# Norm's factor moved from the MLP's up projection to its down projection's sums, in a two-layer encoder trunk

## The chip, the cores and the metric

The kernel runs on one core of a Trainium2 chip. The metric is the device time of one execution in microseconds, as the median of several runs. The engines are TensorE (PE; its weight loads are listed apart as PEld), VectorE (DVE), ScalarE (ACT), GpSimd (POOL) and SyncE (SP), which only issues transfers.

## The reference, cut to what matters

Two layers, each an attention (of different kinds) and an MLP, on 768 tokens of 1024 features; then a last Norm. The MLP is the part that the change touches:

```python
def rmsnorm(x, g, eps=NORM_EPS):
    xf = x.astype(jnp.float32)
    y = xf * lax.rsqrt(jnp.mean(xf * xf, axis=-1, keepdims=True) + eps)
    return (y * g.astype(jnp.float32)).astype(x.dtype)
...
        h = rmsnorm(x, ln_mlp[layer])
        x = x + jnp.square(jax.nn.relu(h @ w_up[layer])) @ w_down[layer]
    return rmsnorm(x, ln_f)
```

The up projection goes from 1024 to 4096 features, the down projection back. Norm's factor, call it R, is one positive number for each token. So relu(R u) squared is R squared times relu(u) squared, and a factor of a token can be taken through the down projection, which sums over features.

## The kernel before, in words

**Layout and arithmetic.** Everything lies with features on the 128 partitions and tokens along the free axis: x is 8 tiles of 128 x 768. `A` is the first half of the tokens, `B` the second, 384 each. Each fp32 operand is split in a high and a low half (`wsplit`, L76 to L81, for weights: ScalarE copies the high half `whi`, VectorE subtracts for `wlo`; `halve`, L114 to L120, for the other operand), and each product is made as three matmuls: high times high, high times low, low times high.

**Seven products for eight.** Both projections multiply 2 x 2 blocks by a scheme of the Strassen-Winograd kind: seven products of sums of blocks, and sums of the products afterwards. `comb` holds the sums of x for the up projection: 0 to 3 are plain blocks (`first`, L799), 4 to 7 sums (`second`, L804).

**Up projection** (L899 to L955). 16 steps over `mp`, each with 256 of the 4096 features. The first two are made with eight plain products, since the sums are not ready; in the others `weights` (L825) loads two tiles `wraw` (three buffers), GpSimd makes four sums of weights (L846), and the halves go through four buffers each of `whi` and `wlo`. The seven products go in the order 1, 3, 2, 6, 4, 7, 5 (L931 to L951); VectorE folds them from PSUM into `z` (L941 to L953). Then `finish` (L875): VectorE makes relu and the multiplication by R in one pass over 128 x 1536 (L880), ScalarE squares (L882), VectorE makes the sums of the four blocks of z that the down projection's products need (`t`, L889 to L891), and ScalarE's and GpSimd's queues store them to a DRAM tensor `T` (L883, L893). Norm's squares and their sum over features (`nm.add`, L141) come at the start, `rstd` (L155) and the spread of R over the partitions (L170) after the first blocks; so `finish` of the first two blocks waits until step 2.

**Down projection** (L959 to L1057). 28 steps: seven products in the order 1, 2, 7, 4, 5, 6, 3 (`ORDER`, L965), each over four groups `i` of features; a step has 48 matmuls into four PSUM banks (r = 0 to 3, L1022). SyncE loads weight blocks three steps ahead (`fetch`, L972), tiles that are kept and changed by later sums in pool `ch`, the others in `wd`, some in `wraw`. GpSimd adds a new block to a kept one for products 7, 5, 6 and 3 (`sums`, L987), two steps ahead; `halves` (L993) splits them one step ahead. `operand` (L920) reads a block of T back and splits it. After the last step of a product its four banks are folded into x, which holds the residual (L1029 to L1048); `u` keeps products 1 + 6.

**Behind it.** In layer 0 the next layer's split and Norm squares follow (L1061 to L1069). In layer 1 `final` (L1071) makes the last Norm for one half of the tokens while product 3 runs and for the other half at the end.

**Order.** The program text gives priorities; a scheduler orders each engine's instructions before the run by its own estimate of times and by which buffers are free. Each engine then runs its list strictly in that order, so an instruction that waits holds up all behind it on its engine.

Of the kernel before, what the change touches and what calls it, by code (L numbers as in the profile page):

```python
# [11 lines left out]
F32 = mybir.dt.float32  # L12
# [25 lines left out]
def kernel(ctx: ExitStack, tc: tile.TileContext, a: dict, y: bass.AP):  # L38
# [735 lines left out]
    def mlp(layer, src, o, x, es):  # L774
# [6 lines left out]
        sq = lambda: xo_tile("sq")  # L781
        two = [0]

        def sq2():
            two[0] ^= 1
            return xo_tile("sq") if two[0] else cpool.tile([P, NT], F32, tag="R", name="sq", bufs=1)

        nm = Norm(sq2)
# [82 lines left out]
        R, wait, done = [], [], list(range(FF // 256))  # L871

        T = [dram.tile([P, 7, ND, HT], F32, name=f"T{layer}_{i}") for i in range(NG)]

        def finish(z):  # L875
# [4 lines left out]
            nc.vector.scalar_tensor_tensor(out=z, in0=z, scalar=0.0, in1=R[0][:, None, :].broadcast_to([P, 2, NT]),  # L880
                                           op0=ALU.max, op1=ALU.mult)
            nc.scalar.activation(z, z, AF.Square)  # L882
# [17 lines left out]
        for k in MO:  # L900
            nm.add(x[k])
        for w in ws:
            z = ztile()
            pss = [bank(n) for n in (1, 6, 2, 4)]
            for last, bs in enumerate((((0, 0, 1), (0, 0, 0), (1, 1, 2), (1, 1, 3)), ((0, 1, 2), (0, 1, 3), (1, 0, 1), (1, 0, 0)))):
                for n, (i, j, c) in enumerate(bs):
                    product(pss[n], w[i, j], c, last == 0, last == 1)
                if last == 0 and wait:
                    rt = nm.rstd()
            for n, (i, sl) in enumerate(((0, B), (0, A), (1, B), (1, A))):  # L910
                nc.scalar.activation(z[:, i, sl], pss[n], AF.Copy)  # L911
            wait.append(z)
            if len(wait) == 1:
                w2 = weights()
                second()
        R.append(nm.spread(rt))
# [11 lines left out]
        for mp in range(2, FF // 256):  # L928
            w = weights() if mp > 2 else w2
# [6 lines left out]
            if mp == FF // 256 - 1:  # L936
# [3 lines left out]
                ths = [operand(1, 0)]  # L940
            add(z12, one(6), z11)  # L941
            add(z11, p2, z11)
            if mp == 2:
                finish(wait.pop(0))
# [4 lines left out]
            if mp == 2:  # L949
# [3 lines left out]
            add(z12, p5, z12)  # L953
            finish(z)
        g2s.close()  # L955
# [43 lines left out]
        def fold(out, x_, op=ALU.add):  # L999
            add(out, out, x_, op)  # L1000

# [6 lines left out]
        for s, (n, i) in enumerate(steps):  # L1008
# [20 lines left out]
            if i == NG - 1:  # L1029
                for r, ps in enumerate(banks):  # L1030
                    x12, x11, x22, x21 = (xb(r, m_, sl) for m_ in PR for sl in (A, B))
                    if n == 1:
                        nc.scalar.activation(u[:, r], ps, AF.Copy)
                    if n in (1, 2):
                        fold(x11, ps)
                    if n == 4:
# [221 lines left out]
```

## Time and profile before

| | us |
|---|---|
| three runs | 1743.85, 1742.30, 1744.41 |
| median | 1743.85 |
| profiled execution, its own time | 1743.15 |
| its span, first to last instruction | 1741.4 |
| up projection, layer 0 (first to last matmul of L861) | 361.8 to 610.3 |
| down projection, layer 0 (L1027) | 610.2 to 847.6 |
| up projection, layer 1 | 1238.4 to 1488.1 |
| down projection, layer 1 | 1487.9 to 1728.1 |

In the lines below, a group reads: line, engine, operation, output<-inputs, shapes, count | busy time in us, mean ns of one | idle time of the engine ahead of them, and what ended it. A timeline line reads: start, length in us, instruction, and in brackets the idle time before it and what ended that. A row of windows reads: stretch, length, busy time and number of instructions for PE, PEld, DVE, ACT and POOL, TensorE's granted clock as a share of full speed, the transfer engines' busy share, GB/s.

### The profile page before, as it was taken

Reading aid. Unit: us, or ns where it says so; the run is one execution under the profiler, and the core shown is the slowest. Engines: PE = TensorE matmul, PEld = TensorE weight load, DVE = VectorE, ACT = ScalarE, POOL = GpSimd, SP = SyncE. Lnnn points to the kernel's source line nnn. Section 1 sums busy time; section 2 is a strip of 40 time slices with the busy share of each in tenths; the row PEclk is TensorE's granted clock in tenths of the full one; section 3 lists DMA queues with packets and bytes.
Section 4 is the critical chain, followed back from the end, with each engine's and each line's share of the span. In section 5 each row is a group of like instructions: output and inputs, shape, how many; then the busy total and the mean of one; then the engine's idle time right before and its main releaser. Section 6 shows DMA issues by size and latency. Waiting matters only on the chain.

```text
span 1741.4 us, 28288 instructions
## 1 busy us (share of the span) xinstructions
PE 1710.9 (98%) x10988; PEld 1622.0 (93%) x10988; DVE 1396.1 (80%) x2202; ACT 823.5 (47%) x1513; POOL 571.3 (33%) x435
## 2 busy tenths in 40 slices
PE   8999999999999999999999999999999999999997
PEld 8888888899999999999999999988999999999997
DVE  8888647499888888899566776775898898787994
ACT  7765434354333354444435555554543333544442
POOL 2200000034566414574021222210235655054751
PEclk9999999999999999999999999999999999999998
DMA  4111222414444687663310111112134445977621
GB/s 170 37 46 49 69 78 91 136 38 156 158 158 157 199 343 300 244 209 133 115 49 32 50 39 33 55 59 97 49 117 160 159 168 177 345 294 266 207 91 73
DMA packets 74597, 235.42 MB, mean 135 GB/s; under 512 B 7904, under 2 KB 25056, under 8 KB 74464
## 3 DMA queue, kind: packets, MB, share of 16 engines
q1 hardware_dynamic: 52480, 186.93, 31.4%
q0 software_dynamic: 7168, 25.17, 3.9%
q10 hardware_dynamic: 14816, 21.52, 3.4%
q8 instruction: 86, 1.41, 0.3%
q14 instruction: 47, 0.39, 0.1%
HBM read 182.47 MB, written 50.33 MB: 134 GB/s over the span
## 4 chain that ended last, share of the span: by engine, by line
PE 69%; DVE 19%; issue 6%; ACT 4%; POOL 1%; DMA 1%; POOLq 0%; DVEq 0%; ACTq 0%; SPq 0%
PE dn L1027 26%; PE dqk L196 8%; PE opa L208 5%; DVE z L880 4%; PE dvp L196 4%; DVE z L869 3%; DVE wlo L81 3%; PE npa L208 3%; PE opb L208 3%; DVE t L869 3%; DVE t L797 2%; ACT z L882 2%; PE ds L274 2%; PE dpv L721 2%; PE qp L196 2%
## 5 line engine op out<-in xcount | busy, mean ns | idle before, releaser
L861 PE MATMUL up<-c,whi 128*128 128x384 f32 x1824 | 467.3, 337 | 1.3 <-ACT z L911 1.3
L1027 PE MATMUL dn<-th,whi 128*128 128x384 f32 x1792 | 460.8, 338 | 0.0
L861 PEld LDWEIGHTS up<-c,whi 128*128 128x128 f32 x1824 | 330.3, 188 | 1.6 <-ACT z L911 1.5
L1027 PEld LDWEIGHTS dn<-th,whi 128*128 128x128 f32 x1792 | 325.7, 188 | 0.7 <-DVE th L117 0.5
L861 PE MATMUL up<-c,wlo 128*128 128x384 f32 x912 | 309.8, 340 | 4.9 <-DVE wlo L81 4.7
L1027 PE MATMUL dn<-th,wlo 128*128 128x384 f32 x896 | 302.9, 338 | 0.5 <-DVE wlo L81 0.5
L846 POOL TENSOR_TENSOR s<-wraw 128x512 f32<-128x512 f32 x56 | 104.1, 1877 | 420.3 <-DMA wraw<-in_w_up_dram 369.6
L991 POOL TENSOR_TENSOR ch<-ch,wd 128x1024 f32<-128x1024 f32 x60 | 189.1, 3161 | 117.0 <-DVE wlo L81 94.5
L81 DVE TENSOR_TENSOR wlo<-ch,whi 128x1024 fp32r<-128x1024 f32 x88 | 167.2, 1915 | 27.7 <-ACT whi L80 27.5
L861 PEld LDWEIGHTS up<-c,wlo 128*128 128x128 f32 x912 | 171.3, 188 | 12.4 <-DVE wlo L81 12.1
L80 ACT ACTIVATE whi<-ch 128x1024 fp32r<-128x1024 f32 x88 | 93.2, 1064 | 176.2 <-PE dn L1027 138.9
L1027 PEld LDWEIGHTS dn<-th,wlo 128*128 128x128 f32 x896 | 168.3, 188 | 1.1 <-DVE wlo L81 1.1
L117 DVE TENSOR_TENSOR th<-tr,th 128x1536 fp32r<-128x1536 f32 x56 | 142.3, 2544 | 12.0 <-ACT th L116 11.5
L81 DVE TENSOR_TENSOR wlo<-wraw,whi 128x1024 fp32r<-128x1024 f32 (+3 forms) x132 | 139.2, 1055 | 14.3 <-ACT whi L80 14.1
L80 ACT ACTIVATE whi<-wraw 128x1024 fp32r<-128x1024 f32 (+3 forms) x128 | 116.8, 914 | 55.3 <-PE opb L208 24.6
L882 ACT ACTIVATE z<-z 128x1536 f32<-128x1536 f32 x32 | 47.7, 1490 | 165.8 <-DVE z L880 165.8
L196 PE MATMUL dqk<-whi,xh 128*128 128x256 f32 x384 | 114.7, 299 | 0.0
L196 PE MATMUL dqk<-whi,xl 128*128 128x256 f32 x384 | 107.5, 280 | 0.0
L196 PE MATMUL dqk<-wlo,xh 128*128 128x256 f32 x384 | 107.2, 279 | 0.0
L706 ACT ACTIVATE de<-ds,m 128x512 f32<-128x512 f32 (+1 forms) x96 | 58.4, 613 | 81.7 <-DVE m L704 81.7
L116 ACT ACTIVATE th<-tr 128x1536 fp32r<-128x1536 f32 x56 | 82.7, 1477 | 23.2 <-DMA tr<-T 14.1
L869 DVE TENSOR_TENSOR z<-up,z 128x384 f32<-128x384 f32 x168 | 89.7, 548 | 0.1
(220 smaller groups left out, 3736.4 us busy)
## 6 DMA issues: line engine op xcount, KB each, us to landing
wd<-in_w_down_dram SPq DMA_DIRECT2D x84, 512.0 KB, 5.0
tr<-T SPq DMA_DIRECT2D x56, 768.0 KB, 5.6
wraw<-in_w_up_dram SPq DMA_DIRECT2D x64, 512.0 KB, 3.6
T<-t POOLq DMA_DIRECT2D x64, 384.0 KB, 3.0
T<-z ACTq DMA_DIRECT2D x32, 576.0 KB, 3.0
ch<-in_w_down_dram SPq DMA_DIRECT2D x28, 512.0 KB, 7.4
wraw<-in_w_in_o_dram SPq DMA_DIRECT2D x24, 512.0 KB, 3.6
wraw<-in_w_in_e_dram SPq DMA_DIRECT2D x16, 512.0 KB, 3.6
```

What stands on the lines that cost most here:

```text
L80: nc.scalar.activation(hi, raw, AF.Copy)
L81: nc.vector.tensor_tensor(out=lo, in0=raw, in1=hi.bitcast(F32), op=ALU.subtract)
L116: nc.scalar.activation(hi, src, AF.Copy)
L117: nc.vector.tensor_tensor(out=lo, in0=src, in1=hi.bitcast(F32), op=ALU.subtract)
L196: nc.tensor.matmul(ps[:, :256], st[:, tk], col(k, part, 0, 256), start=(k == 0 and i == 0), stop=(k == KD - 1 and i == 2))
L208: nc.tensor.matmul(ps[:, : e - s], w, mv[:, s:e], start=(k == 0 and i == 0), stop=(k == nk - 1 and i == 2))
L846: nc.gpsimd.tensor_tensor(out=d_, in0=x_, in1=y_, op=ALU.add)
L861: nc.tensor.matmul(ps, part[a_][:, base + k * P : base + (k + 1) * P], t[:, b_], start=start and k + i == 0, stop=stop and k == 3 and i == 2)
L869: nc.vector.tensor_tensor(out=out, in0=x_, in1=y_, op=op)
L882: nc.scalar.activation(z, z, AF.Square)
L991: nc.gpsimd.tensor_tensor(out=t, in0=t, in1=new.pop((i, rp)), op=ALU.add)
L1027: nc.tensor.matmul(ps, w[a_][:, c : c + P], th[:, b_, q], start=i + q + a_ + b_ == 0, stop=i == NG - 1 and q == ND - 1 and a_ == 1)
```

## The change

R no longer appears in `finish`. The fold into z ends with two passes on ScalarE, Relu and Square, on the whole tile (in the first two blocks Relu is made as the copy out of PSUM). Norm's squares are added one tile a step in steps 4 to 11, its factor is made in step 12, and after the loop the factor is spread and squared to `R2`. In the down projection the products run in the order 4, 5, 6, 3, 1, 7, 2. Their sums are gathered in `e`, `f` and `h` without the factor; when one of them is complete it is multiplied by R2 and then added to x: `e` after product 1, `h` and `f` after product 7; products 1 and 2 go through a tile `t` to the fourth part. Product 4's weight blocks now come first and are kept for 5, 6 and 3. The last Norm begins with the half A, since B is last to be complete, and takes its temporary tiles from `e`. `sq2` moves to the end of layer 0.

```diff
@@ up projection @@
-        nm = Norm(sq2)
+        nm = Norm(lambda: cpool.tile([P, NT], F32, tag="R", name="sq", bufs=1))
...
+        def square(z, relu=True):
+            if relu:
+                nc.scalar.activation(z, z, AF.Relu)
+            nc.scalar.activation(z, z, AF.Square)
 
         def finish(z):
...
-            nc.vector.scalar_tensor_tensor(out=z, in0=z, scalar=0.0, in1=R[0][:, None, :].broadcast_to([P, 2, NT]),
-                                           op0=ALU.max, op1=ALU.mult)
-            nc.scalar.activation(z, z, AF.Square)
...
         ws = [weights(True) for _ in range(2)]
-        for k in MO:
-            nm.add(x[k])
-        for w in ws:
+        for n_, w in enumerate(ws):
...
-                if last == 0 and wait:
-                    rt = nm.rstd()
             for n, (i, sl) in enumerate(((0, B), (0, A), (1, B), (1, A))):
-                nc.scalar.activation(z[:, i, sl], pss[n], AF.Copy)
+                nc.scalar.activation(z[:, i, sl], pss[n], AF.Relu)
+            square(z, False)
...
-        R.append(nm.spread(rt))
...
-                ths = [operand(1, 0)]
+                ths = [operand(4, 0)]
...
             add(z12, p5, z12)
+            square(z)
             finish(z)
+            if 4 <= mp < 4 + KD:
+                nm.add(x[MO[mp - 4]])
+            elif mp == 4 + KD:
+                rt = nm.rstd()
+
+        R2 = cpool.tile([P, NT], F32, tag="R", name="R2", bufs=1)
+        for c in (0, 4):
+            pb = nm.bcast(rt, c)
+            nc.scalar.activation(R2[:, c * P : c * P + pb.shape[1]], pb, AF.Square)
         g2s.close()
@@ down projection @@
-        u = acs.tile([P, 4, HT], F32, name=f"u_{layer}")
+        e, f, h = (acs.tile([P, 4, HT], F32, name=f"{n}_{layer}") for n in "efh")
         PR = (0, 1)
-        ORDER = (1, 2, 7, 4, 5, 6, 3)
+        ORDER = (4, 5, 6, 3, 1, 7, 2)
...
-                if n in (1, 4) and (n, i) != (1, 0):
+                if n in (1, 4) and (n, i) != (4, 0):
                     t = ch.tile([P, 1024], F32, tag="ch", name="ch", bufs=8)
                 else:
-                    third[0] += n != 1
-                    if n == 1 or third[0] % 3 == 0:
+                    third[0] += n != 4
+                    if n == 4 or third[0] % 3 == 0:
                         t = wpool.tile([P, 1024], F32, tag="wraw", name="wd", bufs=3)
...
+        def scaled(out, x_, sl):
+
+            rr = R2[:, sl] if len(x_.shape) == 2 else R2[:, None, sl].broadcast_to([P, 4, HT])
+            nc.vector.tensor_tensor(out=out, in0=x_, in1=rr, op=ALU.mult)
...
                 for r, ps in enumerate(banks):
-                    x12, x11, x22, x21 = (xb(r, m_, sl) for m_ in PR for sl in (A, B))
+                    if n == 4:
+                        nc.scalar.activation(f[:, r], ps, AF.Copy)
+                    if n == 5:
+                        nc.scalar.activation(h[:, r], ps, AF.Copy)
+                    if n == 3:
+                        add(e[:, r], ps, h[:, r])
+                    if n in (6, 1, 7):
+                        fold(f[:, r], ps, ALU.subtract)
+                        fold(h[:, r], ps)
                     if n == 1:
-                        nc.scalar.activation(u[:, r], ps, AF.Copy)
+                        fold(e[:, r], ps)
                     if n in (1, 2):
-                        fold(x11, ps)
...
+                        t = acs.tile([P, HT], F32, tag="t", name="t", bufs=4)
+                        scaled(t, ps, B)
+                        fold(xb(r, 0, B), t)
+                if n == 1:
+                    scaled(e, e, A)
+                    for r in range(4):
+                        fold(xb(r, 0, A), e[:, r])
+                if n == 7:
+                    scaled(h, h, A)
+                    for r in range(4):
+                        fold(xb(r, 1, A), h[:, r], ALU.subtract)
+                    scaled(f, f, B)
+                    for r in range(4):
+                        fold(xb(r, 1, B), f[:, r])
-            if layer == 1 and n == 3 and i < NG - 1:
+            if layer == 1 and n == 2 and i < NG - 1:
                 last[0](i)
-            elif layer == 1 and n == 6 and i == NG - 1:
-                last = [final(x, lambda: acs.tile([P, HT], F32, tag="sq", name="sq", bufs=4), s_) for s_ in (HT, 0)]
+            elif layer == 1 and n == 7 and i == NG - 1:
+                tiles = iter([(e, r) for r in range(4)] * 4)
...
+                last = [final(x, sq, s_, R2[:, A]) for s_ in (0, HT)]
```

More of the change, by code (lines that the diff above doesn't have):

```diff
@@ L926, in operand @@
             return th
-        for mp in range(2, FF // 256):
-            w = weights() if mp > 2 else w2
+        for mp in range(first_mp, FF // 256):
+            w = weights() if mp > first_mp else w2
             one = lambda n: product(bank(n), w[n], n)
@@ L948, in mlp @@
             add(z12, p3, z12)
-            if mp == 2:
+            if wait:
                 finish(wait.pop(0))
@@ L1061, in mlp, with sq2 @@
         es = open_hl()
+        two = [0]
+        def sq2():
+            two[0] ^= 1
+            return xo_tile("sq") if two[0] else cpool.tile([P, NT], F32, tag="R", name="sq", bufs=1)
         nxt, nn = [None] * KD, Norm(sq2)
```

48 lines of the change are left out of this document (16 added, 32 removed).

## The prediction

> **What bounds the kernel now.** I read the page first: its head for TensorE's share, then the groups for TensorE's idle time.
>
> ```profile
> span 1741.4 us, 28288 instructions
> PE 1710.9 (98%) x10988; PEld 1622.0 (93%) x10988; DVE 1396.1 (80%) x2202; ACT 823.5 (47%) x1513; POOL 571.3 (33%) x435
> ...
> L861 PEld LDWEIGHTS up<-c,whi 128*128 128x128 f32 x1824 | 330.3, 188 | 1.6 <-ACT z L911 1.5
> L1027 PEld LDWEIGHTS dn<-th,whi 128*128 128x128 f32 x1792 | 325.7, 188 | 0.7 <-DVE th L117 0.5
> L861 PEld LDWEIGHTS up<-c,wlo 128*128 128x128 f32 x912 | 171.3, 188 | 12.4 <-DVE wlo L81 12.1
> L1027 PEld LDWEIGHTS dn<-th,wlo 128*128 128x128 f32 x896 | 168.3, 188 | 1.1 <-DVE wlo L81 1.1
> ```
>
> TensorE is the bound of the whole. The weight loads carry its idle time better than the matmuls, whose ends are modelled. In the two up projections they stand idle 1.6 + 12.4 = 14.0 us, nearly all behind VectorE's low half of the weights; in the two down projections 0.7 + 1.1 = 1.8 us. The change leaves the number of matmuls as it is, so 15.8 us is all that it can win on this path.
>
> Next the windows, then the groups of 400 to 600 us, which lies in layer 0's loop over blocks. One iteration (a round) is seven products, 84 matmuls.
>
> ```profile
> 400.00:600.00 200.00, 197.44 (x1114) 193.52 (x1113) 180.25 (x207) 77.25 (x87) 112.08 (x76) 1.00 0.48 163
> ```
>
> ```profile
> L880 DVE SCALAR_TENSOR_TENSOR z<-z,R 128x1536 f32<-128x1536 f32 x14 | 36.5, 2612 | 0.0
> L869 DVE TENSOR_TENSOR t<-z 128x768 f32<-128x768 f32 x14 | 22.4, 1600 | 18.7 <-ACT z L882 18.7
> ...
> L882 ACT ACTIVATE z<-z 128x1536 f32<-128x1536 f32 x14 | 20.9, 1492 | 79.0 <-DVE z L880 79.0
> ```
>
> The columns are length, then PE, PEld, DVE, ACT, POOL, clock. The window holds 1114/84 = 13.26 rounds of 15.08 us. A weight load takes 193.52/1113 = 0.174 us, so TensorE needs 14.61 us a round. VectorE is busy 180.25/13.26 = 13.59 and waits 18.7/13.26 = 1.41 for ScalarE's square: 15.00 of 15.08. VectorE, with that wait in it, sets the round. The timeline shows how.
>
> ```profile
> 511.43 2.85 DVE L880 SCALAR_TENSOR_TENSOR z<-z,R 128x1536 f32<-128x1536 f32 x1
> 515.83 1.80 DVE L869 TENSOR_TENSOR t<-z 128x768 f32<-128x768 f32 x1 [1.56 <-ACT z L882]
> ...
> 518.74 0.55 DVE L869 TENSOR_TENSOR z<-up,z 128x384 f32<-128x384 f32 x1
> 519.20 1.21 DVE L81 TENSOR_TENSOR wlo<-wraw,whi 128x1024 fp32r<-128x1024 f32 x1
> ```
>
> ```profile
> 520.47 0.19 PEld L861 LDWEIGHTS up<-c,wlo 128*128 128x128 f32 x1 [0.63 <-DVE wlo L81]
> ```
>
> L880, the wait and the t sums hold VectorE from 511.43; the next round's weight half (519.20) ends as TensorE has already stood 0.63 us for it.
>
> **Up projection.** L880 goes from VectorE (2.75 us a round). ScalarE gets a Relu pass on the same tile. Its price is not in the trace; the square on that shape, 1492 ns, is the nearest row (below it no row reaches for 1536 elements; above it twice that would still leave ScalarE under two thirds full). The Norm's adds move from the start into rounds 4 to 11, one each:
>
> ```profile
> L152 DVE TENSOR_TENSOR acc<-acc,sq 128x768 f32<-128x768 f32 x7 | 8.7, 1239 | 0.2
> ```
>
> VectorE's work becomes 13.59 - 2.75 = 10.84 us, 12.08 with an add; its wait grows from 1.41 to 1.41 + 1.49 = 2.90 at most. Together 13.74 in six of fourteen rounds, below 14.61; with the add 14.98 if nothing fills the wait, 13.74 if the add, which does not need the square, does. ScalarE goes from 77.25/13.26 = 5.8 to 7.3 us a round, plus about a us for the Norm's square in eight: half a round. Queued behind t on VectorE are the folds of the next round and its weight halves, whose customer is TensorE; the T stores on POOL's queue and ScalarE's come by the same route and have no one waiting in the loop.
>
> At the start, the factor's broadcast also costs TensorE time (layer 1):
>
> ```profile
> 1274.35 1.42 PEld L185 LDWEIGHTS pb<-ident,rt 128*128 128x128 f32 x12 [1.03 <-POOL rt L167]
> 1277.28 0.30 PEld L861 LDWEIGHTS up<-c,whi 128*128 128x128 f32 x2 [1.51 <-ACT z L911]
> ```
>
> The 1.42 us of small products only move behind the loop; the waits of 1.03 and 1.51 go, since rt is then four rounds old. Of the 14.0 us I take 12.5 as won, leaving 1.5 for round 2, which still finishes two blocks more, and for single rounds. Bounds: 0 to 14.0.
>
> [...] The row: a 1536-element pass takes 1492 ns on ScalarE, 2612 ns on VectorE. [...]
>
> **Into the down projection.**
>
> ```profile
> 612.40 1.76 DVE L880 SCALAR_TENSOR_TENSOR z<-z,R 128x1536 f32<-128x1536 f32 x1
> 619.55 0.19 PEld L1027 LDWEIGHTS dn<-th,wlo 128*128 128x128 f32 x1 [0.56 <-DVE wlo L81]
> ```
>
> VectorE loses 1.76 us ahead of the half that TensorE waits 0.56 for, twice in the kernel: -1.0 (0 to -1.8). Product 4 first in place of 1: same loads, same number of operand reads from SyncE's queue; its last operand now is one that POOL's queue stores, behind t, which is no later than before since z is done earlier.
>
> **Down projection.** POOL's weight sums for the second product are new; before, the second product needed none and those of the third ran during the second:
>
> ```profile
> 653.71 13.00 POOL L991 TENSOR_TENSOR ch<-ch,wd 128x1024 f32<-128x1024 f32 x4 [4.16 <-issue]
> ```
> ```profile
> 610.00:847.00 237.00, 236.76 (x1344) 236.11 (x1344) 210.13 (x151) 109.83 (x102) 102.56 (x34) 1.00 0.64 233
> ```
> ```profile
> wd<-in_w_down_dram SPq DMA_DIRECT2D x84, 512.0 KB, 5.0
> ```
>
> They need tiles one product earlier: 8 sums of 13.00/4 = 3.25 us, 26 us in a product of 33.7 (237 us / 7; a step is a quarter of it). Two wraw buffers now hold block 22 through four products, so every third tile passes through one buffer: 5.0 + 3.25 = 8.3 us against 12.6, 1.5 steps of 8.4. That fits; I price it at 0, and at up to 3 us a layer if the loads come late.
>
> Folds, counted from the code per layer: before 48 of VectorE on 128x384; after 60, and three passes of 128x1536 by R2.
>
> ```profile
> L869 DVE TENSOR_TENSOR x<-x,dn 128x384 f32<-128x384 f32 x32 | 16.4, 543 | 0.0
> L117 DVE TENSOR_TENSOR th<-tr,th 128x1536 fp32r<-128x1536 f32 x28 | 71.4, 2555 | 6.4 <-ACT th L116 6.1
> ```
> ```profile
> 678.00:711.00 33.00, 33.00 (x189) 33.00 (x188) 22.98 (x18) 14.01 (x12) 7.21 (x3) 1.00 0.95 384
> 745.00:779.00 34.00, 34.00 (x195) 34.00 (x195) 34.00 (x19) 14.04 (x12) 26.37 (x8) 1.00 0.60 196
> 779.00:813.00 34.00, 34.00 (x195) 34.00 (x194) 34.00 (x24) 14.89 (x13) 22.15 (x7) 1.00 0.43 143
> 813.00:847.00 34.00, 34.00 (x195) 34.00 (x194) 27.88 (x35) 19.95 (x22) 0.00 (x0) 1.00 0.31 111
> ```
>
> A fold is 16.4/32 = 0.51 us; a scaling pass I price by the operand's pass of that size, 2.55 us. Added: 12 x 0.51 + 3 x 2.55 = 13.8 us a layer, and VectorE has 237 - 210.13 = 26.9 free. What counts is where. The windows while POOL sums are full (34.00 of 34.00), with folds in them, and TensorE lost nothing there: 0.7 + 1.1 us idle in all. The change takes the folds behind products 4 and 5 out of this stretch (copies on ScalarE instead) and halves those behind 6. The new bursts stand behind 1 (24 folds and one pass, 14.8 us) and 7 (16 folds and two passes, 13.3 us). An uncrowded product leaves 33 - 22.98 = 10 us free, and that window held four folds already, by the code; the two bursts bring 28.1 us into two such windows and the last one. Before, 16 folds (8.2 us) behind 6 passed without a stall. I take 1.0 us for both layers; bounds 0 to 10.
>
> **Ends.** In layer 0, R2 stays in use until the last fold, so the next Norm's squares that use this buffer come later.
>
> ```profile
> 851.70 0.95 DVE L152 TENSOR_TENSOR acc<-acc,sq 128x768 f32<-128x768 f32 x1
> 860.05 0.16 DVE L166 TENSOR_SCALAR ms<-ss 128x6 f32<-128x6 f32 x1 [4.94 <-PE ss L161]
> ```
>
> Between the last add and the sum's use lie 860.05 - 852.65 = 7.4 us: two adds of 0.95 with what feeds them fit. In layer 1 the last product's fold becomes a scaling and an add.
>
> ```profile
> 1728.09 0.55 DVE L869 TENSOR_TENSOR x<-x,dn 128x384 f32<-128x384 f32 x1 [0.41 <-PE dn L1027]
> ```
>
> One such pass more on the path to the end: +0.55.
>
> **Sum.** Against the profiled execution, 1743.15 us (1741.4 span and 1.75 around it): -12.5 - 1.0 + 1.0 + 0.55 = -11.95, hence 1731.2. That execution lies 0.70 under the median of 1743.85, so the median should be 1731.9.
>
> **Rivals.**
> - *Bursts in the down projection eat it.* If POOL's sums for 7 fall beside the burst behind 1, that product needs what a crowded one needs, 34 us, and 14.8 more; what half-loaded windows behind it do not absorb stalls TensorE. At the bound of 5 us a layer: 1731.9 + 9 = 1741. For: 14.8 is nearly double the 8.2 seen. Against: sums ran one product ahead of use (653.71 lies in the product before). Chance 0.10.
> - *The wait takes L880's place.* VectorE waits for two passes with nothing filling it: eight rounds of 14.98, 0.37 over the floor, two layers: +5.9, 1737.8. For: the 1.41 us a round stand unfilled today. Against: the add is free to move in. Chance 0.14.
> - *Slower: ScalarE puts a weight copy ahead of Relu.* Such a copy took 1055 ns:
>
> ```profile
> 517.26 1.05 ACT L80 ACTIVATE whi<-s 128x1024 fp32r<-128x1024 f32 x1
> 520.80 1.21 DVE L81 TENSOR_TENSOR wlo<-s,whi 128x1024 fp32r<-128x1024 f32 x1
> ```
>
>   Two such copies, and the wait is 2.90 + 2.10 = 5.00: rounds of 15.84, and 17.08 with the add. It decides once the wait passes 15.08 - 10.84 = 4.24 us (3.00 in the eight rounds). Price over the floor: 2 x (6 x 1.23 + 8 x 2.47) = 54 us at worst; with one copy 2 x (6 x 0.18 + 8 x 1.42) = 25. With the one: 1743.85 + 25 - 14.0 - 1.0 + 1.55 = 1755. Against: the copies need buffers that TensorE frees at different times, and t's wait need not be ahead of the halves. Chance 0.07.
> - *The change does not touch the stall.* If raw loads and POOL's sums set the round, nothing is won: 1744 or 1745. Against: the copy of the sum was done at 518.3, its low half began at 520.80, so VectorE was late, not the sum. Chance 0.05.
>
> **Numbers.** Forecast 0.64, for which 1728 to 1735 is the likeliest stretch. A measurement tells about 0.2%, 3.5 us, from no change: faster ends at 1740.4, slower begins at 1747.3. Faster: 0.64 + 0.14 + half the first rival 0.05 = 0.83; same: 0.05 + 0.05 = 0.10; slower 0.07. Low end: all 15.8 won with 0.55 added, 1743.85 - 15.25 = 1728.6, and 1.6 for the spread of runs below their median (1742.3): 1727. High end 1740 takes in the second rival and part of the first.
>
> **What would show it.** Right: the up projection's weight loads idle under 2 us for wlo; VectorE's busy time in the loop near 11 to 12 us a round; rounds of 14.6 to 14.7; the down projection's loads still idle under 3 us. Wrong: t waiting over 4 us for the square, rounds at 15 us, or down weight loads idle over 5 us behind wlo at the starts of products 7 and 2.

## The result: a little slower, and the profile after

| us | before | after |
|---|---|---|
| median of four runs each | 1744.13 (1742.30 to 1744.86) | 1754.66 (1753.00 to 1756.60) |
| ratio, 95% interval | | 1.0061 [1.0045, 1.0077] |
| profiled execution, its span | 1743.15, 1741.4 | 1753.98, 1752.2 |
| start of the first up matmul, layer 0 | 361.77 | 363.65 |
| up projection, layer 0 / layer 1 | 248.21 / 249.41 | 245.66 / 246.04 |
| from its end to the down projection | 0.18 / 0.17 | 1.43 / 1.43 |
| down projection, layer 0 / layer 1 | 237.08 / 239.77 | 241.63 / 246.05 |
| between the layers | 391.11 | 391.55 |
| last down matmul to the end | 13.66 | 14.77 |

A stage runs here from the start of its first matmul to the start of its last. The rows say where the 10.8 us between the spans are: the up projections, with the 1.25 us of small products that now stand behind each, won 3.4 us where 12.5 were forecast; the down projections lost 10.8; the end lost 1.1, and the start, whose code is the same, 1.9. The ratios of the runs below leave out two slow executions, one of the kernel before (1846.23 us) and one of e2_up_alone (3181.11 us).

The groups of the page after that answer to the four shown of before (the matmul lines are now L854 and L1034):

```profile
L854 PEld LDWEIGHTS up<-c,whi 128*128 128x128 f32 x1824 | 332.1, 189 | 6.5 <-ACT whi L80 6.4
L1034 PEld LDWEIGHTS dn<-th,whi 128*128 128x128 f32 x1792 | 326.7, 188 | 1.8 <-DVE th L117 1.8
...
L1034 PEld LDWEIGHTS dn<-th,wlo 128*128 128x128 f32 x896 | 168.8, 188 | 9.3 <-DVE wlo L81 9.3
L854 PEld LDWEIGHTS up<-c,wlo 128*128 128x128 f32 x912 | 172.4, 189 | 1.9 <-DVE wlo L81 1.9
```

The wait that the change was to remove went: 12.4 us for wlo in the up projections became 1.9. But 6.4 us for ScalarE's high halves (`whi`) are new there, and the down projections went from 0.7 + 1.1 to 1.8 + 9.3 us.

The loop itself does what was forecast. The window of its later rounds (columns as before: length, PE, PEld, DVE, ACT, POOL, clock):

```profile
415.00:600.00 185.00, 185.00 (x1065) 185.00 (x1064) 136.71 (x178) 89.74 (x89) 95.58 (x73) 1.00 0.51 166
```
```profile
L862 DVE TENSOR_TENSOR t<-z 128x768 f32<-128x768 f32 x13 | 14.0, 1075 | 22.3 <-ACT z L871 22.3
```

TensorE has no gap in 185 us; 1065/84 = 12.68 rounds of 14.59 us, VectorE busy 10.8 us in each. It waits 22.3/12.68 = 1.8 us a round for the square, where up to 2.9 were forecast. All that the up projection lost was lost in one place ahead of this window. The timeline of the weight loads there, then those of ScalarE and VectorE:

```profile
406.65 0.30 PEld L854 LDWEIGHTS up<-c,whi 128*128 128x128 f32 x2 [3.03 <-ACT whi L80]
407.91 0.29 PEld L854 LDWEIGHTS up<-c,wlo 128*128 128x128 f32 x1 [0.96 <-DVE wlo L81]
408.08 0.65 PEld L854 LDWEIGHTS up<-c,whi 128*128 128x128 f32 x2
...
411.50 0.36 PEld L854 LDWEIGHTS up<-c,whi 128*128 128x128 f32 x2
```
```profile
402.94 0.85 ACT L147 ACTIVATE sq<-x 128x768 f32<-128x768 f32 x1 [1.70 <-DVE acc L152]
...
404.81 0.84 ACT L147 ACTIVATE sq<-x 128x768 f32<-128x768 f32 x1 [0.65 <-DVE acc L152]
405.56 1.04 ACT L80 ACTIVATE whi<-s 128x1024 fp32r<-128x1024 f32 x1
```
```profile
401.96 0.94 DVE L152 TENSOR_TENSOR acc<-acc,sq 128x768 f32<-128x768 f32 x1
403.82 0.96 DVE L152 TENSOR_TENSOR acc<-acc,sq 128x768 f32<-128x768 f32 x1 [0.91 <-ACT sq L147]
...
405.75 0.95 DVE L152 TENSOR_TENSOR acc<-acc,sq 128x768 f32<-128x768 f32 x1
```

These are Norm's squares and their additions (L147, L152). The text has them in steps 4 to 11; here, in round 2, the last of them run. They go through one buffer, so each square waits for the addition of the one before, and the copy `whi<-s`, for which TensorE stands, is queued on ScalarE behind two of them, which stand 1.70 + 0.65 us waiting and take 1.69. Layer 1 shows the same at 1287.30, with 3.41 us.

The third line shows a second loss: from 407.6 on two weight loads take 0.65 us together, where they take 0.36 at 411.50. The granted clock of this stretch:

```profile
407.00:411.00 4.00, 3.36 (x12) 3.09 (x11) 3.54 (x5) 3.52 (x4) 0.63 (x1) 0.57 0.51 186
```

In the record of the clock it is at half for 3.41 us; half of that, some 1.7 us, is my estimate of what TensorE loses by it. The changed kernel has four such stretches, at 32.1, 407.6, 1288.2 and 1547.6; the kernel before has none ahead of its last microseconds.

In the down projection the loads stop at three places in products 4 and 5, and once behind product 1 (layer 0 shown; layer 1 stops for 1.01, 0.84, 2.18 and 1.63 us at the same places):

```profile
637.00 0.19 PEld L1034 LDWEIGHTS dn<-th,whi 128*128 128x128 f32 x1 [0.82 <-DVE th L117]
...
654.80 0.19 PEld L1034 LDWEIGHTS dn<-th,wlo 128*128 128x128 f32 x1 [0.80 <-DVE wlo L81]
...
665.37 0.19 PEld L1034 LDWEIGHTS dn<-th,wlo 128*128 128x128 f32 x1 [2.17 <-DVE wlo L81]
...
794.72 0.19 PEld L1034 LDWEIGHTS dn<-th,wlo 128*128 128x128 f32 x1 [1.64 <-DVE wlo L81]
```
```profile
632.99 3.96 DVE L117 TENSOR_TENSOR th<-tr,th 128x1536 fp32r<-128x1536 f32 x1
...
644.09 3.43 DVE L81 TENSOR_TENSOR wlo<-wd,whi 128x1024 fp32r<-128x1024 f32 x1
```
```profile
644.00:678.00 34.00, 31.68 (x179) 31.04 (x178) 34.00 (x12) 14.69 (x16) 30.21 (x10) 1.00 0.63 232
...
777.00:795.00 18.00, 16.69 (x95) 16.36 (x94) 18.00 (x30) 7.47 (x7) 0.00 (x0) 1.00 0.18 50
```

In the first window VectorE is full with twelve instructions and makes nothing but halves: an operand takes it up to 3.96 us and a weight tile up to 3.43, and GpSimd is adding weights in 30.21 of the 34 us. In the second it is full with thirty instructions while GpSimd rests: there it is the burst of folds behind product 1.

### The profile page after: what moved, and what is told of

Its sections match the earlier page's. It is cut to its first block, busy times and chain, and to the rows that moved or that the text cites. A ratio compares the mean times of both kernels' runs of the same rounds, so it can differ in the third digit from the quotient of the medians.

```text
span 1752.2 us, 28363 instructions
## 1 busy us (share of the span) xinstructions
PE 1713.0 (98%) x10988; PEld 1629.6 (93%) x10988; DVE 1350.9 (77%) x2196; ACT 870.4 (50%) x1553; POOL 550.7 (31%) x435
## 4 chain that ended last, share of the span: by engine, by line
PE 86%; DVE 9%; issue 2%; ACT 1%; DMA 1%; POOL 0%; POOLq 0%; SPq 0%; DVEq 0%; ACTq 0%
PE up L854 24%; PE dn L1034 21%; PE dqk L196 8%; PE opa L208 5%; PE dvp L196 4%; PE npa L208 3%; PE opb L208 3%; DVE wlo L81 2%; PE ds L274 2%; PE dpv L721 2%; PE qp L196 2%; PE vp L196 2%; DVE t L790 1%; PE gs L274 1%; PE npb L208 1%
## 5 line engine op out<-in xcount | busy, mean ns | idle before, releaser
L854 PE MATMUL up<-c,whi 128*128 128x384 f32 x1824 | 469.3, 339 | 5.8 <-ACT whi L80 5.8
L1034 PE MATMUL dn<-th,whi 128*128 128x384 f32 x1792 | 461.5, 339 | 1.2 <-DVE th L117 1.2
L854 PEld LDWEIGHTS up<-c,whi 128*128 128x128 f32 x1824 | 332.1, 189 | 6.5 <-ACT whi L80 6.4
L1034 PEld LDWEIGHTS dn<-th,whi 128*128 128x128 f32 x1792 | 326.7, 188 | 1.8 <-DVE th L117 1.8
L854 PE MATMUL up<-c,wlo 128*128 128x384 f32 x912 | 308.8, 339 | 1.3 <-DVE wlo L81 1.3
L1034 PE MATMUL dn<-th,wlo 128*128 128x384 f32 x896 | 302.9, 339 | 7.3 <-DVE wlo L81 7.3
L839 POOL TENSOR_TENSOR s<-wraw 128x512 f32<-128x512 f32 x56 | 84.2, 1505 | 430.9 <-DMA wraw<-in_w_up_dram 379.7
L993 POOL TENSOR_TENSOR ch<-ch,wd 128x1024 f32<-128x1024 f32 x52 | 168.8, 3261 | 92.8 <-DVE wlo L81 76.5
L81 DVE TENSOR_TENSOR wlo<-ch,whi 128x1024 fp32r<-128x1024 f32 x80 | 161.3, 2044 | 27.0 <-ACT whi L80 26.8
L1034 PEld LDWEIGHTS dn<-th,wlo 128*128 128x128 f32 x896 | 168.8, 188 | 9.3 <-DVE wlo L81 9.3
L854 PEld LDWEIGHTS up<-c,wlo 128*128 128x128 f32 x912 | 172.4, 189 | 1.9 <-DVE wlo L81 1.9
L81 DVE TENSOR_TENSOR wlo<-wraw,whi 128x1024 fp32r<-128x1024 f32 (+3 forms) x132 | 151.8, 1151 | 18.5 <-ACT whi L80 17.7
L80 ACT ACTIVATE whi<-ch 128x1024 fp32r<-128x1024 f32 x80 | 84.8, 1062 | 142.7 <-PE dn L1034 98.5
L80 ACT ACTIVATE whi<-s 128x1024 fp32r<-128x1024 f32 x56 | 59.5, 1063 | 118.5 <-PE up L854 115.6
L81 DVE TENSOR_TENSOR wlo<-s,whi 128x1024 fp32r<-128x1024 f32 x56 | 80.7, 1441 | 46.0 <-ACT whi L80 45.9
```

The source lines that it names most:

```text
L80: nc.scalar.activation(hi, raw, AF.Copy)
L81: nc.vector.tensor_tensor(out=lo, in0=raw, in1=hi.bitcast(F32), op=ALU.subtract)
L839: nc.gpsimd.tensor_tensor(out=d_, in0=x_, in1=y_, op=ALU.add)
L854: nc.tensor.matmul(ps, part[a_][:, base + k * P : base + (k + 1) * P], t[:, b_], start=start and k + i == 0, stop=stop and k == 3 and i == 2)
L993: nc.gpsimd.tensor_tensor(out=t, in0=t, in1=new.pop((i, rp)), op=ALU.add)
L1034: nc.tensor.matmul(ps, w[a_][:, c : c + P], th[:, b_, q], start=i + q + a_ + b_ == 0, stop=i == NG - 1 and q == ND - 1 and a_ == 1)
```

## The experiments

The theory after the result (A): three things cost the time, each by itself, and the exchange of work between VectorE and ScalarE in the loop is sound. First, Norm's squares run as a chain through one buffer at the start of the up projection and delay round 2. Second, in the new order GpSimd's sums begin with the first product and slow VectorE's halves before it has any lead. Third, the burst behind product 1. The rivals were that ScalarE's extra pass costs the time, that the early squares cost it by their mere place, and that the loss lies in the clock alone. The kernel before, beside the runs of the first four experiments, took 1742.26 us (25 runs), beside the next four 1742.18 (21 runs), beside e9 1741.24 and beside e10 1742.55 (13 runs each).

**e1_gate.** The squares go behind the square of their own step:

```diff
+        gate = [None]
         def square(z, relu=True):
...
-            nc.scalar.activation(z, z, AF.Square)
+            gate[0] = nc.scalar.activation(z, z, AF.Square)
...
-                nm.add(x[MO[mp - 4]])
+                with tc.issue_after(gate[0].ins):
+                    nm.add(x[MO[mp - 4]])
```

> The changed kernel, but each of Norm's eight squares is queued on ScalarE behind the square of z of its own step (4 to 11), so that the scheduler cannot pull them ahead into the first three steps. Theory A (in the changed kernel TensorE stands 3.03 us in layer 0, and about as long in layer 1, behind a weight copy on ScalarE that stands behind Norm's squares, which wait for VectorE's adds through their one buffer; the half-speed clock of 3.4 us that follows comes from that stop): both stops and the half-speed stretches behind them go, 5 to 5.5 us a layer, so 1754.7 - 10.5 = about 1744. Rival (ScalarE is late because of the Relu and Square passes of the first blocks, Norm's squares only happen to stand there): the stops stay, 1753 to 1755.

1741.64 us (10 runs), ratio to before 0.9997 [0.9988, 1.0006]. Each up projection takes 240.38 us, 5.3 and 5.7 less than in the changed kernel; the loads of its page:

```profile
L854 PEld LDWEIGHTS up<-c,whi 128*128 128x128 f32 x1824 | 330.4, 188 | 0.1
...
L854 PEld LDWEIGHTS up<-c,wlo 128*128 128x128 f32 x912 | 171.3, 188 | 0.0
```

Where the squares stand is worth 11 us. The down projections still lose what they lost (241.66 and 245.62 us).

**e2_up_alone.** The changed kernel up to the end of the up projection, then the down projection, the last Norm and the order of before. The factor is applied nowhere, so the output is another one.

> The up projection of the changed kernel with the down projection, the order of products and the last Norm of the kernel before; Norm's factor of the MLPs is made and squared but applied nowhere, so this part of the computation is left out. Theory A (the loop of the up projection gains what was forecast, its start loses part of it, the rest of the loss lies in the down projection): up projections 245.7 and 246.0 us as in the changed kernel, the 1.3 us of the factor's small products between the projections, down projections back at 237 and 240: about 1744.1 - 3.4 - 1 = 1740. Rival (the up projection is what makes the kernel slower, by later stores of z or a colder clock): over 1748.

1739.42 us (10 runs), ratio 0.9986 [0.9977, 0.9996]. The up projections are those of the changed kernel (245.94 and 245.90), the down projections take 236.44 and 239.12, 0.6 less each than before. So the loss in the down projections is of their new order and sums, not of what the up projection hands over.

**e3_old_order.** The changed kernel with products in the old order, R2 still applied to the sums, and the two scalings of the last pair moved into product 3:

```diff
-        ORDER = (4, 5, 6, 3, 1, 7, 2)
+        ORDER = (1, 2, 7, 4, 5, 6, 3)
...
+                        nc.scalar.activation(e[:, r], ps, AF.Copy)
+                    if n == 7:
+                        add(h[:, r], ps, e[:, r])
+                    if n == 4:
+                        add(f[:, r], ps, h[:, r], ALU.subtract)
+                    if n in (5, 6):
                         fold(e[:, r], ps)
+                        fold(h[:, r], ps)
...
+            if n == 3 and i == 0:
+                scaled(h, h, A)
...
+            if n == 3 and i == 1:
+                scaled(e, e, A)
```

> The changed kernel with the products of the down projection in the order of before (1, 2, 7, 4, 5, 6, 3); the factor is still applied to sums (13 folds per bank row and three passes by R2; h and e are scaled one and two steps behind product 6). Theory A (the stops of 0.8 to 2.2 us in products 4 and 5, 3.8 us a layer, come from GpSimd's sums for the second product, which now run beside the start of the projection and halve VectorE's speed before it has any lead): these stops go, and the half-speed stretch at 1547 with them, about 9 us; what the bursts behind product 6 cost, 0 to 4, comes in: 1745 to 1749. Rival (VectorE has too much to do in the down projection in any order, with 16 folds and three passes more): the stops move behind product 6 and stay 4 us a layer or more, 1752 or over.

1744.22 us (10 runs), ratio 1.0010 [1.0000, 1.0019], a little under what was expected. The down projections take 236.44 and 239.11 and have no stop. In the projections the factor on the sums, its passes included, is free in the old order; the new order is what costs there. The end is 3.0 us longer than before (16.62 against 13.66 from the start of the last down matmul): TensorE waits 3.04 us there for the last addition of the squares.

**e4_late_scaling.** Only the burst behind product 1 is spread: `e` is scaled and added one step later.

```diff
-                if n == 1:
-                    scaled(e, e, A)
-                    for r in range(4):
-                        fold(xb(r, 0, A), e[:, r])
...
+            if n == 7 and i == 0:
+                scaled(e, e, A)
+                for r in range(4):
+                    fold(xb(r, 0, A), e[:, r])
```

> The changed kernel, but e is scaled and added to x one step later (behind the first step of product 7 instead of behind the last of product 1), so that the weight halves of the next step come before these 3.7 us on VectorE. Theory A (the stop of 1.65 us in product 7's second step, both layers, is the burst of 20 folds and the scaling ahead of that step's low half): the stop goes, 1754.7 - 3.3 = 1751.4. Rival (the 20 folds alone make it late): stays within 1 us of 1754.7.

1750.96 us (4 runs), ratio 1.0047 [1.0031, 1.0064]. The stops of 1.64 and 1.63 us behind product 1 are gone; those in products 4 and 5 stay, in layer 1 as two (1.50 and 2.17 us) in place of three. The burst is one of the three terms. Its size, 3.3 us by the stops, is less sure: the same edit on e1 (e6, below) gives 1741.64 - 1739.39 = 2.3 us.

**e5_gate_old_order.** e1 and e3 together.

> Norm's squares held in their own steps (as in e1_gate) and the old order of products (as in e3_old_order) together. Theory A (the two losses are separate, and the gain of the up projection's loop is what the prediction said): the up projections take 240.4 us each as in e1_gate, the down projections 236.4 and 239.1 us as in e3_old_order, so about 1744.2 - 5.5 - 6.7 = 1732 to 1734, which is where the prediction put the changed kernel. Rival (the gains overlap, or a tighter up loop leaves the down projection less lead): 1738 or over.

1733.54 us (5 runs, 1731.96 to 1734.50), ratio 0.9946 [0.9932, 0.9959]: faster than both kernels, by 8.6 us than the one before. The loads wait nowhere in the four projections:

```profile
L854 PEld LDWEIGHTS up<-c,whi 128*128 128x128 f32 x1824 | 330.4, 188 | 0.1
...
L1037 PEld LDWEIGHTS dn<-th,whi 128*128 128x128 f32 x1792 | 325.9, 188 | 0.0
...
L1037 PEld LDWEIGHTS dn<-th,wlo 128*128 128x128 f32 x896 | 168.2, 188 | 0.0
```

**e6_gate_late_scaling.** e1 and e4 together.

> Norm's squares held in their own steps and e scaled one step later, in the order of products of the changed kernel. Theory A (losses add): 1741.6 - 3.3 = 1738, and what is left against e5_gate_old_order, about 5 us, is the stops in products 4 and 5. Rival (they overlap): 1741 or more.

1739.39 us (10 runs), ratio 0.9985 [0.9976, 0.9994], 1.4 over the expected. The stops in products 4 and 5 are there in both layers (0.82, 0.78 and 2.21 us in layer 0), and in both layers the last of them is followed by a stretch at half clock. Against e5 this prices the new order, without its burst, at 5.9 us in all. In the profiled executions its down projections take 9.4 us more (241.15 + 243.81 against 236.44 + 239.11) and its end 2.3 us less (14.30 against 16.63); e5's execution, but not e6's, also lost time to a stretch at half clock at 32 us.

**e7_gate_vector_relu.** e1 with the pass back on VectorE, as a plain maximum without the factor:

```diff
-                nc.scalar.activation(z, z, AF.Relu)
+                nc.vector.tensor_scalar(z, z, 0.0, None, op0=ALU.max)
```

> As e1_gate, with Relu on VectorE (a max with zero in place, one input) instead of ScalarE. [...] Theory A (the loop has about 2 to 4 us a round free on VectorE without the pass; a one-input pass of 128x1536 takes 0.9 to 1.8 us): the up projections stay at 240.4 us within 1 us, so 1741 to 1743; the place of the pass does not matter once the multiplication by R is gone. Rival (VectorE becomes the bound of the loop again): up projections over 244 us, 1748 or more.

1740.42 us (10 runs), ratio 0.9991 [0.9982, 1.0000]; the interval overlaps that of e1. The up projections take 240.27 and 240.38. The loop's window; in it the groups of the pass and of the t sums; and the pass on ScalarE in the changed kernel's window:

```profile
415.00:600.00 185.00, 185.00 (x1065) 185.00 (x1064) 160.60 (x195) 78.83 (x84) 97.04 (x73) 1.00 0.52 174
```
```profile
L872 DVE TENSOR_SCALAR z<-z 128x1536 f32<-128x1536 f32 x12 | 23.5, 1956 | 0.0
...
L862 DVE TENSOR_TENSOR t<-z 128x768 f32<-128x768 f32 x13 | 19.8, 1522 | 20.2 <-ACT z L873 20.2
```
```profile
L870 ACT ACTIVATE z<-z 128x1536 f32<-128x1536 f32 x13 | 19.4, 1493 | 10.2 <-DVE z L862 10.2
```

VectorE is then busy 160.60/12.68 = 12.7 us a round, and with 20.2/12.68 = 1.6 of waiting for the square ahead of the t sums 14.3 of 14.6: just under the bound. Taking the factor out of the pass was enough; to move the pass gave room and no time. The mean of 1956 ns mixes two kinds: the passes beside GpSimd's sums take 2.05 us, the one in this window without a sum beside it 0.95 (0.9 to 1.8 was the estimate).

**e8_gate_no_sums.** e1 without GpSimd's weight sums in the down projection (the kept tiles are used as they are, so the output is another). One run.

```diff
-                    nc.gpsimd.tensor_tensor(out=t, in0=t, in1=new.pop((i, rp)), op=ALU.add)
+                    new.pop((i, rp))
```

> As e1_gate, with GpSimd's sums of the down projection's weights left out (the products 5, 6, 3 and 7 use the kept block unchanged, so these products are not those of the reference). Theory A (the sums beside VectorE's two-input passes are what makes the halves late in products 4 and 5): the stops of 0.87, 0.78 and 2.22 us (layer 0) and 0.86, 0.86 and 2.19 us (layer 1) go, the operand pass of 128x1536 takes 1.75 us everywhere instead of 2.53 on average, the stop of 1.65 behind product 1 stays, since no sums run there: about 1741.6 - 8 = 1734. Rival (the operands and weights arrive late because the transfers are full there): the stops in products 4 and 5 stay.

1741.84 us. The stops in products 4 and 5 are gone, and VectorE's halves take half as long:

```profile
630.78 1.76 DVE L117 TENSOR_TENSOR th<-tr,th 128x1536 fp32r<-128x1536 f32 x1 [0.75 <-ACT th L116]
633.02 1.23 DVE L81 TENSOR_TENSOR wlo<-wd,whi 128x1024 fp32r<-128x1024 f32 x1 [0.48 <-ACT whi L80]
```
```profile
637.00:671.00 34.00, 34.00 (x195) 34.00 (x195) 16.76 (x12) 15.85 (x18) 0.00 (x0) 1.00 0.90 322
```

Twelve passes of the same kinds take VectorE 16.76 us in place of 34.00. The stop of 1.63 us behind product 1 stays, as it should. The time did not follow to 1734: TensorE stops 4.0 and 2.5 us at the start of the two down projections for ScalarE's half of the first operand, which no other kernel here does. In layer 0 SyncE's queue issues that operand's load at 602.71, behind five loads of weight blocks; in e1 it does so at 592.98, behind two. So the run shows what slows the halves and causes the stops in products 4 and 5; its time does not price them. From their first matmul on, its down projections take 239.59 and 240.73 us, 2.1 and 4.9 less than e1's, though the first holds a stretch of 3.41 us at half clock that e1's does not.

**e9_two_buffers.** The changed kernel with Norm's squares going through two buffers in turn, as before:

```diff
-        nm = Norm(lambda: cpool.tile([P, NT], F32, tag="R", name="sq", bufs=1))
+        two = [0]
+
+        def sq2():
+            two[0] ^= 1
+            return xo_tile("sq") if two[0] else cpool.tile([P, NT], F32, tag="R", name="sq", bufs=1)
+
+        nm = Norm(sq2)
```

> The changed kernel with one edit: the squares of Norm go through two buffers in turn again, as in the kernel before, instead of one; they still stand early, in the first three rounds of the loop of the up projection. Theory A (each square waits for VectorE's addition of the one before, because of the one buffer, and the weight copy of the third round stands behind this chain): with two buffers ScalarE runs one addition ahead, the stop of 3.03 us ahead of the third round in layer 0 and of 3.4 us in layer 1 falls below 1 us, the half-speed stretch of 3.4 us behind it goes in at least one layer, and the time falls by 4 to 8 us from 1753.98, to 1746 to 1750. Rival (the squares cost the round simply because they are there, 0.84 us of ScalarE each, whatever buffer they use): the stop stays at 2 us or more in both layers, and the time stays at 1752 to 1755.

1742.98 us (10 runs), ratio 1.0011 [1.0002, 1.0021]; the up projections take 240.38 us each, and there is no stop in round 2. That is more won than expected (1746 to 1750), and the premise was wrong: the squares do not stand early in this kernel.

```profile
356.49 0.83 ACT L147 ACTIVATE sq<-x 128x768 f32<-128x768 f32 x1
...
450.59 0.85 ACT L147 ACTIVATE sq<-x 128x768 f32<-128x768 f32 x1 [2.22 <-DMA T<-t]
```

The second buffer is one that the t sums use too, and comes free when their store to T has landed; so the squares wait for that, into rounds 5 and later. The run shows what placed them early in the changed kernel (a buffer that nothing else holds), but does not tell the chain from the place. The next one takes the chain away.

**e10_squares_only.** The changed kernel in which seven of the squares are made but not added (so the factor is that of one tile):

```diff
-                nm.add(x[MO[mp - 4]])
+                if mp == 4:
+                    nm.add(x[MO[0]])
+                else:
+                    nc.scalar.activation(nm.temp(), x[MO[mp - 4]], AF.Square)
```

> The changed kernel, in which seven of Norm's eight squares in the up projection are still made on ScalarE but no longer added on VectorE (so the factor is that of one tile, and the output is another). The squares keep their one buffer and are placed even earlier, all ahead of the third round's weight copy, but nothing makes one wait for the other. Theory A (it is the chain of square, addition, square on one buffer that delays the weight copy): the stop ahead of the third round, 3.03 us in layer 0 and 3.4 in layer 1, falls below 1 us, each up projection takes 240 to 241.5 us against 245.66 and 246.04, and the time is 1742 to 1746. Rival (it is the early place: 0.84 us of ScalarE each, ahead of the copies that TensorE waits for): each up projection still takes 244 us or more, and the time stays at 1750 to 1755.

1741.30 us (10 runs), ratio 0.9994 [0.9984, 1.0003]. The up projections take 240.38 us each, without a stop. ScalarE's timeline:

```profile
356.66 1.71 ACT L952 ACTIVATE sq<-x 128x768 f32<-128x768 f32 x2
...
364.93 1.71 ACT L952 ACTIVATE sq<-x 128x768 f32<-128x768 f32 x2
```

All squares run by 366.6, earlier than ever, and cost nothing. Without the chain (a square, an addition on another engine, the next square, with TensorE's weight copy queued in between) the early squares are harmless. As they also moved, ahead of the busy rounds, the run does not price them unchained at 402.9 to 405.65; there, by the timeline above, the waits of 1.70 and 0.65 us are the chain's and the squares' own 1.69 us are not. The time fell a little below the expected range: its profiled execution has no stretch at half clock ahead of the last microseconds. Its down projections still take 241.62 and 244.31 us, with the stops, so the loss does not lie in the clock alone.

## Why the prediction was wrong

**The loop (right).** VectorE at 10.8 us a round and rounds of 14.6 came as worked out, without the adds, which ran ahead of the loop; with the adds in their rounds (e1) the up projections have no stop either. The wait for two ScalarE passes filled itself in part with other work (1.8 us of up to 2.9 stayed). With the stop taken away (e1, e9, e10) the two up projections, with the 1.25 us of small products that moved behind each, take 14.4 us less than before, where 12.5 were taken.

**"The Norm's adds move from the start into rounds 4 to 11, one each" (the first step that failed).** I took the place in the text for the place in the engines' lists. The scheduler put the squares where a buffer allowed. With the two buffers of before, one of them shared with the T stores, the squares stay in rounds 5 and later (e9); the changed kernel sends them all through R's buffer, which the change itself had left idle during the loop. So they ran at the start, in the rounds where ScalarE and VectorE are busy with the sums of x, as a chain between the two. I had let ScalarE's squares count as half a round of work and no wait. Cost: 245.66 + 246.04 - 2 x 240.38 = 10.9 us.

**"I price it at 0" for GpSimd's sums (the second).** My reason was about transfers: would the tiles come in time. The transfers did; the halves did not: the page puts the 1.8 + 9.3 us of stops down to VectorE, which is busy in all 34.00 us from 644 on. I had read the full windows of before (34.00 of 34.00) as work that fits, since TensorE lost nothing there. They fitted with GpSimd adding in 22 to 26 us of each 34. The window of before at the place of the one shown of after:

```profile
644.00:678.00 34.00, 34.00 (x195) 34.00 (x194) 32.08 (x18) 14.28 (x13) 21.86 (x7) 1.00 0.69 242
```

There the sums start 36 us into the stage, and VectorE has room for 18 instructions. In the new order they start 8.5 us into it, at 619.20, in the first product, and three products' sums run nearly back to back (30.21 of 34). An operand's pass then takes up to 3.96 us and a weight tile's up to 3.43, against 1.76 and 1.23 without sums (e8): 2.20 us more in both shapes. Counted in the traces, some 60 passes of the two kinds are slowed in the whole kernel, before and after, for 64 sums, none by more than 2.25 us; so a product with eight sums, eight tiles and four operands is about 8 x 1.23 + 4 x 1.76 + 8 x 2.20 = 34.5 us of work in 33.7, an estimate. The slowed passes are not more than before, they come sooner: of the passes that begin in the first 33.9 us of layer 0's stage, none of 15 was slowed before, and 7 of 12 are after.

My rate of 2555 ns for an operand's pass was a mean over both kinds; it also overpriced the passes by R2, which take 1.75 us where no sums run. Cost: the stops are 0.82 + 0.80 + 2.17 in layer 0 and 1.01 + 0.84 + 2.18 in layer 1, 7.8 us, and 1.7 for the half clock behind the last. To take the folds out of this stretch did not help, since halves alone fill it. That the missing lead counts beside the density of the sums is my reading of these counts; the runs show the order (e3) and the sums (e8), not these two apart.

**Fold bursts at 1.0 (mechanism right, size off).** The stop is behind wlo in product 7, as named, though in its second step and not at its start, and measures 1.64 + 1.63 = 3.3 us; e4 removes both. The rival's cause, sums beside this burst, was not there (POOL 0.00 in that window). Product 2's start, also named, has no stop.

**Into the down projection (right).** -1.0 was taken; e5 against before gives 0.64 + 0.66 = 1.3 us.

**The end.** +0.55 was taken, 1.1 came: 1.4 and 0.8 us of waiting for the last additions and squares, where 1.17 were waited before.

**The clock (not in the sum).** Each stop was costed at its own length. In the changed kernel's profile three in the two projections were followed by 3.41 us at half clock, by the estimate above 1.7 us more each; the stretch at 32 us in unchanged code belongs to this, below.

**The rivals.** The slower rival's 1755 is near the time measured, but its mechanism was another: it had weight copies ahead of Relu make VectorE late in every round, and what came was a weight copy behind Norm's squares in one round of sixteen, with the rest of the loss in the down projection. The number was right by accident. Which of the two engines makes Relu does not show in the time: the pass takes 1493 ns on ScalarE, on VectorE 2.05 us beside GpSimd's sums and 0.95 without them (e7), and e7 and e1 do not differ.

With both failed steps repaired, e5 wins 1742.18 - 1733.54 = 8.6 us of the 12.0 forecast. In its profile the up projections win 14.4 and the down projections 1.3, the end loses 3.0, and the start 3.4, with a stretch of 6.83 us at half clock in unchanged code. The first half of the change was worth what was said; the second half's order took it back.

## What to carry to other kernels

When an edit frees a buffer or drops a wait, ask what the scheduler will now move forward into the gap, and whether that work passes back and forth between two engines whose queues hold TensorE's operands. A full engine that stalls no one may have no slack to lend; if the order of stages changes, count which of its passes will now meet the neighbour's work, and what lead it has by then. And test a change of two halves as halves: e2 and e3 showed in two runs which half to keep.

## What the runs showed of the hardware that was not expected

**VectorE's passes beside GpSimd's sums.** In the down projections of the kernels before and after, VectorE's halves, both of whose inputs lie in SBUF, take up to 3.97 instead of 1.76 us (128x1536) and up to 3.45 instead of 1.22 (128x1024) when GpSimd adds 128x1024; each of the slowed ones meets a sum. In e5 the eight additions `x<-x,t` of 128x384 between 640 and 820 us, where sums run, take 1.03 us in the mean; in the changed kernel, without a sum beside them, 0.54 to 0.56. The loss is up to about 2.2 us in both shapes of the halves, so it looks like a wait for the sum that is running, and not like a slower rate: in the changed kernel a sum runs from 660.33 for 3.90 us, and the weight tile's pass that begins at 661.92 takes 3.40 and ends 1.09 behind it; the pass that begins at 690.33, ahead of a sum at 690.49, takes 1.21. The sums lose too: that one takes 3.33 us, where one of 128x1024 that meets no such pass takes 2.40 (739.35); the longest takes 3.94. Folds, with one input in PSUM, take the same in both cases: in the kernel before, the 38 that meet a sum 0.54 to 0.56 us, the 34 others of the same size 0.54 to 0.56. The pass that the change removed, also with two inputs, shows it in the lines of before: 2.85 us in the loop (511.43), 1.76 at 612.40, where GpSimd rests. A pass with one input in SBUF is not spared either: the maximum of e7 takes 2.05 us beside sums and 0.95 without.

**Half clock behind some stops, and not behind others.** In the up projections, stops of 3.03 to 3.41 us came with a stretch at half clock each time (the changed kernel, e2, e3, e4), of 3.41 us, or of 6.83 in e3's layer 1 and in both layers of e4. One of 2.6 to 2.7 us at 32 us, in the same code of every kernel, was followed by it in some executions only (3.41 us in the changed kernel, e2, e8 and e9, 6.83 in e1, e4 and e5, none in the kernel before, e3, e6, e7 and e10). Windows of that stretch, before and after:

```profile
32.00:36.00 4.00, 4.00 (x36) 4.00 (x36) 3.83 (x24) 2.78 (x10) 3.06 (x9) 1.00 0.00 0
```
```profile
32.00:36.00 4.00, 3.79 (x20) 3.83 (x20) 3.83 (x23) 2.95 (x9) 3.15 (x7) 0.57 0.00 0
```

In the changed kernel the stretch stands behind the stop of 2.18 us in layer 1 (a clock of 0.66 in 1547 to 1552) and not behind that of 2.17 in layer 0 (1.00 in 665 to 670). The stop of 2.2 us in product 5 is the same in e6 and e10; e6 shows the half clock behind it in both layers, e10 in neither. The weight loads of e6, then of e10:

```profile
658.33 0.19 PEld L1037 LDWEIGHTS dn<-th,wlo 128*128 128x128 f32 x1 [2.21 <-DVE wlo L81]
...
659.76 0.65 PEld L1037 LDWEIGHTS dn<-th,whi 128*128 128x128 f32 x2
```
```profile
658.51 0.19 PEld L1037 LDWEIGHTS dn<-th,wlo 128*128 128x128 f32 x1 [2.17 <-DVE wlo L81]
...
659.67 0.36 PEld L1037 LDWEIGHTS dn<-th,whi 128*128 128x128 f32 x2
```

All these stretches measure 3.41 us or 6.83. What decides whether one follows, and which of the two, was not shown: stops of 2.2 and 2.7 us stand on both sides. In the projections no stop below 2 us was followed by it. In this kernel, whose TensorE is busy in 98% of the span before, a stop of over 2 us cost, by an estimate, half of the stretch more than its own length: 1.7 us with one of 3.41, 3.4 with one of 6.83, and nothing more with none.
